# A hybrid attention layer on one Trainium2 core: queries and keys are transposed before they are split, x groups are split later, and the work is dealt anew over ScalarE, VectorE and GpSimd

## The chip, the cores and the metric

The kernel runs as one program on one core of a Trainium2 chip. A core has five engines with a queue of instructions each, worked off in order: TensorE (PE in the profile, with its weight loads as PEld), VectorE (DVE), ScalarE (ACT), GpSimd (POOL), and SyncE (SP), which here issues the DMAs. TensorE reads SBUF and writes PSUM; GpSimd works on SBUF alone in this kernel. The metric is device time in microseconds (us) of one execution; lower is better. Of the kernel before there are three timed runs and one profiled execution.

## The reference

One decoder layer on x of 2048 positions and 1024 channels, in float32:

```python
hdn = rmsnorm(x, norm_gain[i])
proj = jnp.einsum("bsd,de->bse", hdn, w_in[i])
q_a, k_a, v_a, g_a, q_b, k_b, v_b, g_b = jnp.split(proj, split_at, axis=-1)

q_a = rope(rmsnorm(q_a.reshape(b, S, A_HEADS, HEAD_DIM), q_norm_a[i]), pos)
k_a = rope(rmsnorm(k_a.reshape(b, S, A_KV_HEADS, HEAD_DIM), k_norm_a[i]), pos)
v_a = v_a.reshape(b, S, A_KV_HEADS, HEAD_DIM)
o_a, _, _ = banded_attention(q_a, k_a, v_a, A_WINDOW - 1, sinks=sinks_a[i])
o_a = o_a.reshape(b, S, A_WIDTH).astype(x.dtype) * jax.nn.silu(g_a)

q_b = rope(rmsnorm(q_b.reshape(b, S, B_HEADS, HEAD_DIM), q_norm_b[i]), pos)
k_b = rope(rmsnorm(k_b.reshape(b, S, B_HEADS, HEAD_DIM), k_norm_b[i]), pos)
v_b = v_b.reshape(b, S, B_HEADS, HEAD_DIM)
o_b = dilated_attention(q_b, k_b, v_b)
o_b = o_b.reshape(b, S, B_WIDTH).astype(x.dtype) * jax.nn.silu(g_b)

mixed = jnp.concatenate([o_a, o_b], axis=-1)
x = x + jnp.einsum("bse,ed->bsd", mixed, w_out[i])
```

Mixer A has 8 query heads and 2 key heads of 64 channels and looks back 127 positions, with a learned sink per head. Mixer B has 8 heads; each attends under three patterns of window and stride, (128, 1), (512, 4) and (2048, 16), and the three results are merged by their softmax denominators.

## The kernel before

**Split products.** TensorE works in the format fp32r, so every float32 operand is split into a high part h (a ScalarE copy into fp32r) and a low part l (the value less h). A projection product is three matmuls, h*h, h*l and l*h (`mm3`, line L244). A score is two: the stationary operand holds the query's high part in 64 of its 128 partitions and its low part in the other 64; the first moving operand holds the key's high part in both halves (tile `KK`), the second the key's low part in the half that meets the query's high part and zeros elsewhere (tile `KLZ`, in the profile `klz`; L590, L591).

**Stages.** `STAGES` has eight: four of kind B (two heads of mixer B each), two of kind A (four query heads and one key head), two of kind O (half of the output columns each). Every stage goes through 2048 positions as four `sb` of 512 and eight halves `hf` of 256. `proj` does a half: two matmul groups `pj` of 128 positions (`tt`), 24 matmuls of 384 columns each, then one (B) or two (A) gate groups of 24 matmuls of 256 columns. `pj` has two PSUM buffers, which the gates use too.

**x.** `x_load` brings eight of the 16 half groups, two of four x groups, into `xs` in one DMA on SP; `x_split` makes `xh` on ScalarE (L155) and `xl` on GpSimd or VectorE (L157): groups 0 and 1, and all of hf 6 and 7, on GpSimd, the rest on VectorE. The tiles `xh` and `xl` have six buffers each; a half needs four. The next half's groups 0 and 1 are split after this half's first `pj` group, groups 2 and 3 during its last gate group.

**Queries and keys.** `norm_rope` multiplies `pj` by the rope tables on VectorE into `t1` (four buffers) and `t2`, and GpSimd adds them (L430). `norm_split` multiplies by the norm factor (L446) and splits at once, positions still on the partitions: high parts on ScalarE (L455, L456), low parts on GpSimd (L457, L458), all into `hl`. The next half's `finish`, taken from `deferred` after its second `pj` group, calls `qk_transposes`: TensorE transposes blocks of `hl` that pair high and low (L474 and L498 in B, L484, L489 and L490 in A) into PSUM tiles `po`, and ScalarE copies them into `Q`, `qc`, `KK` and `KLZ` (L476, L477, L501; in A L486, L492, L493). In B, GpSimd copies the queries into a second layout `qc`, which goes to DRAM for the strided patterns.

**Attention.** Units of scores, transposes of the probabilities, products with the values and a last step wait in `pending`. `proj` yields an estimated cost after each pair of operations, and the main loop starts the next step of a unit whenever the attention's share of work has fallen behind the projection's. `evac_o` and `pair_units` move the products out of PSUM by a ScalarE copy into `ob` (one buffer) and a VectorE add.

**Order.** The program is written in this order, and a scheduler then orders each engine's queue by its own estimates. So where an instruction stands on its engine is read from the compiled order.

## Time and profile before

| what | value |
|---|---|
| three timed runs, median | 1264.9 us (1262.76 to 1270.4) |
| the profiled execution, its own time | 1271.72 us |
| its span, first to last instruction | 1269.9 us |
| mean granted TensorE clock | 0.97 |
| ScalarE, x splits (L155) | 252 of 627 ns |
| VectorE, x splits (L157) | 94 of 859 ns |
| GpSimd, x splits (L157) | 158 of 1365 ns |

Groups of instructions are told by source line, engine, operation, and the tiles written and read. Busy time is that of the group; the idle time beside it is what its engine stood just before, with what ended it. A matmul's own duration includes its way through the array, so that consecutive ones overlap; what one holds of TensorE is the distance from its start to the next one's. A row of waits names the engine and line that waited, and the one whose end released it.

### The profile page before, as it was taken

The numbers are of one execution on the slowest core, as the hardware profiler recorded it, in microseconds if no ns is written. First come the engines' busy times: TensorE is split into PE (matmuls) and PEld (weight loads), VectorE is DVE, ScalarE is ACT, GpSimd is POOL, SyncE is SP. The second block draws the span as 40 slices with busy tenths as digits, with TensorE's granted clock in tenths as the row PEclk, the third lists the DMA queues.
The fourth block names the chain that finished last, engine by engine and source line by source line (L and its number), as shares of the span: only waits on it lengthen the run. The fifth ranks groups of instructions, "written<-read, shape, count | busy, mean of one in ns | idle before, by whom it ended". The sixth has DMA issues, their size and how long they took to land. (4 is left out here: it accounts for less than half of the span.)

```text
span 1269.9 us, 25442 instructions
## 1 busy us (share of the span) xinstructions
PE 1179.8 (93%) x8328; PEld 1143.5 (90%) x8328; DVE 867.5 (68%) x2288; ACT 837.1 (66%) x2418; POOL 685.3 (54%) x788
## 2 busy tenths in 40 slices
PE   6898979988799898898998999999899999999899
PEld 6798979988699898898997999998799998999898
DVE  5666678776667677776877879888777868622221
ACT  6567777777668587676877767786776877513221
POOL 4876644566454755545676566673556565333122
PEclk9899989999999899898998999999899999999999
DMA  7454678776677776787866775555223235566551
GB/s 215 128 148 114 176 214 243 211 202 185 193 212 232 198 198 181 219 235 197 221 200 191 212 199 150 149 165 165 91 73 109 80 97 157 164 197 205 177 188 70
DMA packets 196883, 220.98 MB, mean 174 GB/s; under 512 B 34312, under 2 KB 143632, under 8 KB 196752
## 3 DMA queue, kind: packets, MB, share of 16 engines
q1 hardware_dynamic: 196752, 219.37, 59.2%
q8 instruction: 66, 1.08, 0.4%
q14 instruction: 65, 0.53, 0.1%
HBM read 164.44 MB, written 54.86 MB: 173 GB/s over the span
## 5 line engine op out<-in xcount | busy, mean ns | idle before, releaser
L244 PE MATMUL pj<-wh,xh 128*128 128x384 f32 (+1 forms) x1008 | 334.1, 334 | 18.6 <-ACT xh L155 6.7
L244 PE MATMUL pj<-wl,xh 128*128 128x384 f32 (+1 forms) x1008 | 334.9, 332 | 1.4 <-DVE wl L102 0.8
L244 PE MATMUL pj<-wh,xl 128*128 128x384 f32 (+1 forms) x1008 | 331.9, 331 | 1.1 <-POOL xl L157 0.8
L157 POOL TENSOR_TENSOR xl<-xs,xh 128x512 fp32r<-128x512 f32 x158 | 213.7, 1365 | 143.8 <-ACT xh L155 139.1
L155 ACT ACTIVATE xh<-xs 128x512 fp32r<-128x512 f32 x252 | 153.5, 627 | 115.8 <-PE pj L244 98.8
L244 PEld LDWEIGHTS pj<-wh,xh 128*128 128x128 f32 x1008 | 194.4, 193 | 22.4 <-ACT xh L155 7.1
L244 PEld LDWEIGHTS pj<-wl,xh 128*128 128x128 f32 x1008 | 194.6, 193 | 3.6 <-DVE wl L102 1.1
L244 PEld LDWEIGHTS pj<-wh,xl 128*128 128x128 f32 x1008 | 194.4, 193 | 3.5 <-DVE xl L157 1.3
L574 DVE TENSOR_TENSOR ptl<-pt,pth 128x512 fp32r<-128x512 f32 (+3 forms) x232 | 141.6, 619 | 42.2 <-ACT pth L573 40.2
L244 PE MATMUL pj<-xh,wgh 128*128 128x256 f32 x496 | 147.1, 297 | 10.7 <-DVE V L310 8.4
L244 PE MATMUL pj<-xh,wgl 128*128 128x256 f32 x496 | 145.3, 293 | 0.0
L244 PE MATMUL pj<-xl,wgh 128*128 128x256 f32 x496 | 144.7, 292 | 0.0
L573 ACT ACTIVATE pth<-pt 128x512 fp32r<-128x512 f32 (+3 forms) x232 | 123.1, 543 | 25.6 <-PE po L645 9.4
L430 POOL TENSOR_TENSOR t<-t,t 128x256 f32<-128x256 f32 (+1 forms) x96 | 79.2, 826 | 80.9 <-DVE t L421 57.2
L244 PEld LDWEIGHTS pj<-xh,wgh 128*128 128x128 f32 x496 | 97.7, 197 | 12.9 <-DVE V L310 5.8
L446 DVE TENSOR_TENSOR t<-t,fac 128x256 f32<-128x256 f32 (+1 forms) x96 | 76.9, 815 | 33.0 <-POOL fac L182 30.1
L244 PEld LDWEIGHTS pj<-xh,wgl 128*128 128x128 f32 x496 | 97.7, 197 | 0.8
L814 ACT ACTIVATE P<-P,scD 128x128 f32<-128x128 f32 (+3 forms) x128 | 71.6, 560 | 40.5 <-DVE scD L813 39.6
L244 PEld LDWEIGHTS pj<-xl,wgh 128*128 128x128 f32 x496 | 97.8, 197 | 0.4
L157 DVE TENSOR_TENSOR xl<-xs,xh 128x512 fp32r<-128x512 f32 x94 | 79.8, 859 | 20.2 <-ACT xh L155 19.8
L182 POOL TENSOR_TENSOR fac<-un,mhalf 128x8 f32<-128x8 f32 (+1 forms) x48 | 85.3, 1778 | 2.7
L599 ACT ACTIVATE P<-P,scA 128x256 f32<-128x256 f32 (+1 forms) x128 | 63.1, 495 | 23.4 <-DVE scA L598 23.0
(188 smaller groups left out, 3087.8 us busy)
## 6 DMA issues: line engine op xcount, KB each, us to landing
xs<-in_xT SPq DMA_DIRECT2D x94, 512.0 KB
xs<-mx SPq DMA_DIRECT2D x32, 512.0 KB
vd<-V SPq DMA_DIRECT2D x64, 128.0 KB
qd<-qc SPq DMA_DIRECT2D x32, 256.0 KB
TT<-tab SPq DMA_DIRECT2D x32, 256.0 KB
cv<-vd SPq DMA_DIRECT2D x32, 256.0 KB
cq<-qd SPq DMA_DIRECT2D x32, 256.0 KB
ck<-kd SPq DMA_DIRECT2D x64, 128.0 KB
```

The costliest lines, as they stand in the source:

```text
L155: nc.scalar.activation(h, f, AF.Copy)
L157: eng.tensor_tensor(l, f, f32(h), op=OP.subtract)
L182: nc.gpsimd.tensor_tensor(y, u, mhalf.to_broadcast([128, n]), op=OP.pow)
L244: nc.tensor.matmul(o, a, b, start=first and n == 0, stop=last and n == 2, skip_group_check=True)
L430: nc.gpsimd.tensor_tensor(t1[:, :n], t1[:, :n], t2[:, :n], op=OP.add)
L446: nc.vector.tensor_tensor(t1v, t1v, fac[:, tt, :, None].to_broadcast([128, nh, 64]), op=OP.mult)
L573: nc.scalar.activation(hi, pt, AF.Copy)
L574: nc.vector.tensor_tensor(lo, pt, f32(hi), op=OP.subtract)
L599: nc.scalar.activation(pd, pd, AF.Exp, bias=nb[i], scale=-1.0, accum_out=l[i])
L814: nc.scalar.activation(pd, pd, AF.Exp, bias=nb, scale=-1.0, accum_out=l)
```

## The change

- `norm_split` is gone. `norm_scale` only multiplies `t1` by the norm factor. The unsplit float32 `t1` of a half's two groups goes to `qk_transposes`, and `t1` is held until then.
- `qk_transposes` transposes `t1` with the float32 identity `idf`: four blocks in B, four and two in A (on `t1`'s 64 key columns). One ScalarE copy stages each PSUM tile in SBUF, in a tile named `ob`, which now has two buffers.
- From the staged tile, ScalarE writes the high queries and both copies of the high keys, VectorE subtracts for the low queries (two instructions in B, four in A), and GpSimd subtracts for the low keys (two).
- In A, the low keys lie in both `KLZ` halves, one for even and one for odd heads, so that two query heads can have their high parts in different partitions; the copies at the border of two `sb` are two there, not one.
- `xh` and `xl` have seven buffers. GpSimd subtracts three of four x groups. Group 1 is split during the second `pj` group, group 2 behind it, group 3 in the last gate group; in the O stages groups 1 to 3 during the second group, and both x loads are issued at the start of a half.
- The yields and the cost table `pcost` are adjusted.

```diff
-XB = 6
+XB = 7
...
-        eng = nc.gpsimd if g < 2 or hf >= 6 else nc.vector
+        eng = nc.gpsimd if g < 3 or hf >= 6 else nc.vector
...
+                    if nx and tt == 1 and c == 3:
+                        x_split(*nx, 1)
                     yield 490
                 if tt == 0 and nx:
                     x_load(*nx, 1)
                     x_split(*nx, 0)
-                    x_split(*nx, 1)
...
                 if tt == 1:
+                    if nx:
+                        x_split(*nx, 2)
...
-                    if nx and gc == ngc - 1 and c in (1, 3):
-                        x_split(*nx, 2 + c // 2)
+                    if nx and gc == ngc - 1 and c == 3:
+                        x_split(*nx, 3)
...
+    def qk_transposes(si, sb, half, t1s):
         KK, KL = K[si, sb]
         q = Q[si, sb]
         i0 = 2 * half
+        lo64, hi64 = slice(0, 64), slice(64, 128)
+
+        def keys(t, h):
+            return t[:, h, :, i0 + 1:i0 + 3, :].rearrange("p r i u -> p i r u")
+
+        def queries(tile, h, src):
+            a, b = (hi64, lo64) if h else (lo64, hi64)
+            o = tile[:, h, i0:i0 + 2, :]
+            nc.scalar.activation(o[a], src[a], AF.Copy)
+            nc.vector.tensor_tensor(o[b], src[a], f32(o[a]), op=OP.subtract)
+
+        def staged(pt):
+            f = wk.tile([128, 2, 2, 128], F32, name="ob", bufs=2)
+            nc.scalar.activation(f, pt, AF.Copy)
+            return f
+
+        if STAGES[si][0] == "B":
+            pt = ps.tile([128, 2, 2, 128], F32, name="po", bufs=2)
+            for b in range(2):
+                for tt, t1 in enumerate(t1s):
+                    nc.tensor.transpose(pt[:, b, tt, :], t1[:, 128 * b:128 * b + 128], idf)
+            F = staged(pt)
+            for h in range(2):
+                queries(q[0], h, F[:, 0])
+            pk = F[:, 1].rearrange("p i (r u) -> p i r u", u=32)
+            for h, (a, b) in enumerate(((lo64, hi64), (hi64, lo64))):
+                nc.scalar.activation(keys(KK, h)[a], pk[a], AF.Copy)
+                nc.scalar.activation(keys(KK, h)[b], pk[a], AF.Copy)
+                nc.gpsimd.tensor_tensor(keys(KL, h)[a], pk[a], f32(keys(KK, h)[a]), op=OP.subtract)
...
+            F = staged(pt)
+            for b in range(2):
+                for h in range(2):
+                    queries(q[b], h, F[:, b])
+            yield 436
+            pt = ps.tile([64, 2, 128], F32, name="po", bufs=2)
+            for tt, t1 in enumerate(t1s):
+                nc.tensor.transpose(pt[:, tt, :], t1[:, 256:320], idf)
+            F = wk.tile([64, 2, 128], F32, name="ob", bufs=2)
+            nc.scalar.activation(F, pt, AF.Copy)
+            pk = F.rearrange("p i (r u) -> p i r u", u=32)
+            for a in (lo64, hi64):
+                nc.scalar.activation(keys(KK, 0)[a], pk, AF.Copy)
+            for h, a in enumerate((lo64, hi64)):
+                nc.gpsimd.tensor_tensor(keys(KL, h)[a], pk, f32(keys(KK, 0)[lo64]), op=OP.subtract)
```

**The order at three places.** The number behind a tile's name tells its instances apart.

TensorE before, in the first A stage, the first gate group of the fifth half (`pj_11365`) and the transposes of split data, of two halves before, that fall into it:

```order
L244 MATMUL pj_11365<-xh_10870,wgh_9598 128x256
L244 MATMUL pj_11365<-xl_10871,wgh_9598 128x256
L244 MATMUL pj_11365<-xh_10870,wgl_9599 128x256
L244 MATMUL pj_11365<-xh_10870,wgh_9607 128x256
L244 MATMUL pj_11365<-xl_10871,wgh_9607 128x256
L489 MATMUL po_10975<-idr_76,hl_10744 128x128
L490 MATMUL po_10975<-idr_76,hl_10744 64x128
L484 MATMUL po_10995<-idr_76,hl_10750 128x128 x4
L719 MATMUL pt_11158<-idf_75,P_11033 128x128 x4
```

TensorE after, at the same place: the last transpose of `t1` from two halves before, and then the gate group (`pj_10944`) of this half:

```order
L495 MATMUL po_10587<-idf_75,t1_10154 64x128
L718 MATMUL pt_10733<-idf_75,P_10622 128x128 x4
L670 MATMUL po_10662<-idf_75,eA_10657 8x128
L807 MATMUL sc_10968<-ck_10758,cq_10756 128x256
L808 MATMUL sc_10968<-cl_10761,cq_10756 128x256
L807 MATMUL sc_10977<-ck_10758,cq_10756 128x384
L808 MATMUL sc_10977<-cl_10761,cq_10756 128x384
L734 MATMUL po_10766<-pth_86,V_9332 128x512
L734 MATMUL po_10781<-pth_86,V_9712 128x512
L734 MATMUL po_10781<-pth_86,V_9815 128x256
L734 MATMUL po_10781<-pth_86,V_9406 128x256
L242 MATMUL pj_10944<-xh_10450,wgh_9206 128x256
```

The gate group stood 11 rows ahead of the key transposes (L489, L490); now it begins 11 rows behind them (L495). The rope products of this half, which have to be done before that PSUM buffer is used again, write a `t1` buffer that these transposes read.

VectorE before, in the first A stage, at the rope products (L426, L428) of the sixth half's first 128 positions:

```order
L412 TENSOR_REDUCE un_11556<-sq_11675 128x5
L426 TENSOR_TENSOR t1_11679<-pj_11557,TT_11265 128x256
L428 TENSOR_TENSOR t2_11680<-pj_11557,TT_11265 128x256
L426 TENSOR_TENSOR t1_11679<-pj_11557,TT_11265 128x64
L428 TENSOR_TENSOR t2_11680<-pj_11557,TT_11265 128x64
L310 SCALAR_TENSOR_TENSOR V_11674<-pj_11557,rst_83,V_11674 128x64
```

VectorE after, at the rope products (L427, L429) of the same positions:

```order
L459 TENSOR_TENSOR Q_9920<-ob_10908,Q_9920 64x256 x2
L459 TENSOR_TENSOR qc_9921<-ob_10908,qc_9921 64x256
L427 TENSOR_TENSOR t1_11240<-pj_11122,TT_10836 128x256
L429 TENSOR_TENSOR t2_11241<-pj_11122,TT_10836 128x256
L427 TENSOR_TENSOR t1_11240<-pj_11122,TT_10836 128x64
L459 TENSOR_TENSOR qc_9921<-ob_10908,qc_9921 64x256
L429 TENSOR_TENSOR t2_11241<-pj_11122,TT_10836 128x64
L311 SCALAR_TENSOR_TENSOR V_11235<-pj_11122,rst_82,V_11235 128x64
```

The low queries (L459, four instructions of 64x256) of the half two before now stand before and between the rope products.

ScalarE before, in a B stage, the four x splits (`xh`, L155) of one half among the exponentials (L599):

```order
L155 ACTIVATE xh_6424<-xs_6326 128x512
L599 ACTIVATE P_6270,scB_6068<-P_6270,scB_6068 128x256 x2
L155 ACTIVATE xh_6434<-xs_6326 128x512
L599 ACTIVATE P_6270,scB_6068<-P_6270,scB_6068 128x256 x2
L155 ACTIVATE xh_6590<-xs_6470 128x512
L155 ACTIVATE xh_6594<-xs_6470 128x512
```

ScalarE after, at the like place (x splits L153, exponentials L598, tanh of the gates L335, the staging copy L463):

```order
L153 ACTIVATE xh_6180<-xs_6074 128x512
L598 ACTIVATE P_6018,scB_5830<-P_6018,scB_5830 128x256 x2
L153 ACTIVATE xh_6326<-xs_6206 128x512
L598 ACTIVATE P_6018,scB_5830<-P_6018,scB_5830 128x256 x2
L153 ACTIVATE xh_6364<-xs_6206 128x512
L335 ACTIVATE gz_6197<-G_5630 128x256
L565 ACTIVATE ob_5973<-po_5964 64x512
L463 ACTIVATE ob_6138<-po_6133 128x512
```

The four splits of one half stood within six rows, the third and fourth directly behind one another. Now the first group's split stands nine rows ahead of these rows, and the rows show groups 1, 2 and 3, each with other work between.

More of the change, by code (lines that the diff above doesn't have):

```diff
@@ L50, in hybrid_layer @@
     idf = const.tile([128, 128], F32, name="idf")
-    idr = const.tile([128, 128], F32R, name="idr")
     mk = const.tile([128, 768], F32, name="mk")
@@ L78, in late_constants @@
         nc.sync.dma_start(idf, ident)
-        nc.scalar.activation(idr, idf, AF.Copy)
         nc.sync.dma_start(mk, masks)
@@ L348, in finish @@
                 nc.scalar.activation(KK[:, h, :, 0, :], f32(pk[:, h, :, 4, :]), AF.Copy)
-            for h in range(nk):
+            for h in range(2):
                 hs = slice(64 * h, 64 * h + 64)
                 nc.scalar.activation(KL[hs, h, :, 0, :], f32(pl[hs, h, :, 4, :]), AF.Copy)
-        yield from qk_transposes(si, sb, half, hls)
+        yield from qk_transposes(si, sb, half, t1s)
         if half == 0:
@@ L466, in qk_transposes @@
         i0 = 2 * half
-        for tt, hl in enumerate(hls):
-            i = i0 + tt
-            if kind == "B":
-                blocks = [hl[:, 2 * b:2 * b + 2, :] for b in range(4)]
-                pt = ps.tile([128, 4, 128], F32R, name="po", bufs=2)
-                for b, a in enumerate(blocks):
-                    nc.tensor.transpose(pt[:, b, :], a, idr)
-                pv = f32(pt).rearrange("p h (r u) -> p h r u", u=32)
-                nc.scalar.activation(q[0][:, :, i, :], f32(pt)[:, 0:2], AF.Copy)
-                nc.scalar.activation(KK[:, :, :, i + 1, :], pv[:, 2:4], AF.Copy)
+        lo64, hi64 = slice(0, 64), slice(64, 128)
@@ L495, in qk_transposes @@
[L495 to L503 removed]
+            yield 436
+        else:
+            pt = ps.tile([128, 2, 2, 128], F32, name="po", bufs=2)
+            for b in range(2):
+                for tt, t1 in enumerate(t1s):
+                    nc.tensor.transpose(pt[:, b, tt, :], t1[:, 128 * b:128 * b + 128], idf)
+            F = staged(pt)
+            for b in range(2):
+                for h in range(2):
+                    queries(q[b], h, F[:, b])
+            yield 436
+            pt = ps.tile([64, 2, 128], F32, name="po", bufs=2)
+            for tt, t1 in enumerate(t1s):
+                nc.tensor.transpose(pt[:, tt, :], t1[:, 256:320], idf)
[6 more added lines that the diff above has]
+                nc.gpsimd.tensor_tensor(keys(KL, h)[a], pk, f32(keys(KK, 0)[lo64]), op=OP.subtract)
+            yield 218
@@ L564, in evac_o @@
     def evac_o(po, dst):
-        ob = wk.tile([64, 512], F32, name="ob", bufs=1)
+        ob = wk.tile([64, 512], F32, name="ob", bufs=2)
         nc.scalar.activation(ob, po[64:128, :], AF.Copy)
```

67 lines of the change are left out of this document (12 added, 55 removed).

## The prediction

> **What bounds the kernel now.** I read the page's busy line first, then the stretches of the program, then who waited for whom on the way to TensorE, then the groups of instructions by shape.
>
> The page's line of each engine's busy time, share of the span and instructions:
>
> ```profile
> PE 1179.8 (93%) x8328; PEld 1143.5 (90%) x8328; DVE 867.5 (68%) x2288; ACT 837.1 (66%) x2418; POOL 685.3 (54%) x788
> ```
>
> TensorE (PE) is busy for 93% of the 1269.9 us span, and 90.1 us are left. The same by stretches, each row with the length, then PE, weight loads, VectorE (DVE), ScalarE (ACT) and GpSimd (POOL): the four B stages, the two A stages, a full piece of the A stages, the two O stages (cut at about where the kind changes).
>
> ```profile
> 0.00:673.00 673.00, 609.04 (x4060) 589.20 (x4061) 480.14 (x1262) 486.01 (x1394) 390.34 (x491) 0.95 0.69 196
> 673.00:1045.00 372.00, 356.65 (x2522) 343.53 (x2521) 300.96 (x847) 272.77 (x841) 226.68 (x242) 0.98 0.48 140
> 770.00:820.00 50.00, 48.77 (x355) 46.94 (x354) 44.88 (x133) 38.79 (x125) 33.83 (x38) 1.00 0.52 151
> 1045.00:1270.00 225.00, 214.11 (x1750) 210.76 (x1748) 86.41 (x182) 78.29 (x185) 68.25 (x55) 1.00 0.52 164
> ```
>
> The B stages leave PE 64.0 us idle, the A stages 15.4. In the A stages DVE is the next engine: 81% (300.96 of 372), and 90% from 770 to 820 us, where PE still ran at 98%. So time that leaves PE's queue shortens the program, and DVE decides how much of it in A. The waits that bear on this change, with us in total, times and longest:
>
> ```profile
> POOL xl L157 <- ACT xh L155: 139.1, 37, 9.7
> ACT xh L155 <- PE pj L244: 98.8, 62, 7.4
> PE po L474 <- POOL hl L457: 7.9, 7, 2.0
> PE po L484 <- POOL hl L457: 1.1, 1, 1.1
> PE po L498 <- ACT KK L477: 6.4, 2, 5.5
> PE sc L591 <- ACT klz L501: 1.3, 2, 1.1
> ```
>
> ACT stands 98.8 us, in its order, for PE to free an `xh` buffer, and POOL behind it 139.1; PE itself stands 9.0 us for the low halves that POOL makes ahead of the transposes.
>
> **PE: the transposes.** A B half of 256 positions has 10 transposes of split data before (32 halves), an A half 12 (16 halves): 512. After, 4 and 6 of unsplit f32: 224. What one holds of PE's time is read from the timeline, start to start, with the tail that shows in the longer first matmul behind a run:
>
> ```profile
> 301.62 0.47 PE L474 MATMUL po<-idr,hl 128*128 128x128 f32 x4
> 301.92 0.33 PE L498 MATMUL po<-idr,hl 128*128 128x128 f32 x2
> 302.09 0.35 PE L808 MATMUL sc<-ck,cq 128*128 128x256 f32 x1
> 302.28 0.28 PE L809 MATMUL sc<-cl,cq 128*128 128x256 f32 x1
> ...
> 1089.22 0.28 PE L244 MATMUL pj<-wgh,xl 128*128 128x256 f32 x1
> 1089.34 1.03 PE L719 MATMUL pt<-idf,P 128*128 128x128 f32 x8
> 1090.13 0.37 PE L590 MATMUL sc<-KK,qc 128*128 128x256 f32 x1
> 1090.33 0.28 PE L591 MATMUL sc<-klz,qc 128*128 128x256 f32 x1
> ```
>
> A 256-column matmul takes 0.12 us (1089.22 to 1089.34). Six split transposes: 302.28 - 301.62 - 0.12 = 0.54, 0.090 each. Eight unsplit: 1090.33 - 1089.34 - 0.12 = 0.87, 0.109 each. An unsplit one is dearer, but 512 x 0.090 = 46.1 and 224 x 0.109 = 24.4: **PE loses 21.7 us**, 32 x 0.46 = 14.9 of it in B (0.90 - 0.436 a half) and 16 x 0.43 = 6.8 in A. Nothing hides it where PE is full, so it counts whole.
>
> **DVE: the low queries.** The rows by shape (count, busy us, mean ns, idle before):
>
> ```profile
> L740 DVE TENSOR_TENSOR osum<-po,ob 64x256 f32<-64x256 f32 x64 | 26.4, 413 | 3.6 <-ACT ob L737 3.1
> L331 DVE TENSOR_TENSOR G<-pj,RB 128x256 f32<-128x256 f32 x62 | 25.6, 413 | 5.5 <-PE pj L244 5.4
> L335 DVE SCALAR_TENSOR_TENSOR G<-gz,G 128x256 f32<-128x256 f32 x64 | 47.5, 742 | 9.3 <-ACT gz L334 9.1
> L446 DVE TENSOR_TENSOR t<-t,fac 128x256 f32<-128x256 f32 x64 | 54.1, 860 | 27.8 <-POOL fac L182 27.2 <-POOL t L430 0.6
> L157 DVE TENSOR_TENSOR xl<-xs,xh 128x512 fp32r<-128x512 f32 x94 | 79.8, 859 | 20.2 <-ACT xh L155 19.8
> ```
>
> Sixty-four partitions cost as much as 128 (413 and 413). But with both tensors in SBUF the same 256 elements take 742 and 860, not 413. The change adds 2 such subtractions per B half and 4 per A half: 32 x 2 + 16 x 4 = 128 of 64x256, both inputs in SBUF. I take 0.742, the row that also follows an ACT copy directly: 95.0 us; the ends are 0.413 (52.9) and 0.860 (110.1). The third x group of hf below 6 leaves DVE: 6 x 8 - 1 = 47 instructions (half of the 94) x 0.859 = 40.4. Net +54.6 (12.5 to 69.7). In A: 64 x 0.742 - 12 x 0.859 = +37.2, 301 to 338 of 372, or 91%.
>
> By the Trainium skill ("SBUF — State Buffer", section "SBUF: two separate sides") GpSimd and a two-SBUF-input VectorE instruction take a shared port pair as an exclusive lock for a whole instruction. The gap of 329 ns between the L335 and L331 rows agrees with it. By it the change works against itself, giving both engines more of just such work; as an estimate from that page, a wait of half a POOL split at POOL's 57% share, 0.39 us, would make the 128 cost 103 us in place of 95, which leaves the sum as it is and adds to the first rival below.
>
> **POOL and ACT.** Their rows:
>
> ```profile
> L157 POOL TENSOR_TENSOR xl<-xs,xh 128x512 fp32r<-128x512 f32 x158 | 213.7, 1365 | 143.8 <-ACT xh L155 139.1 <-DMA TT<-tab 2.2
> L457 POOL TENSOR_TENSOR hl<-t,hl 128x128 fp32r<-128x128 f32 x64 | 32.3, 504 | 13.7 <-ACT hl L455 12.2 <-PE pj L244 1.3
> L458 POOL TENSOR_TENSOR hl<-t,hl 128x128 fp32r<-128x128 f32 x64 | 31.5, 492 | 1.5 <-ACT hl L456 0.9 <-PE po L849 0.6
> L457 POOL TENSOR_TENSOR hl<-t,hl 128x256 fp32r<-128x256 f32 x32 | 26.9, 842 | 17.8 <-ACT hl L455 17.8
> L458 POOL TENSOR_TENSOR hl<-t,hl 128x64 fp32r<-128x64 f32 x32 | 13.1, 411 | 0.0
> L566 ACT ACTIVATE ob<-po 64x512 f32<-64x512 f32 x64 | 38.1, 595 | 15.3 <-PE po L849 8.3 <-PE po L645 5.8
> L456 ACT ACTIVATE hl<-t 128x256 fp32r<-128x256 f32 x64 | 26.0, 407 | 0.3
> L455 ACT ACTIVATE hl<-t 128x128 fp32r<-128x128 f32 x64 | 19.4, 303 | 9.7 <-DVE t L446 7.6 <-PE po L498 1.9
> L476 ACT ACTIVATE Q<-po 128x256 fp32r<-128x256 f32 x64 | 24.2, 378 | 11.4 <-PE po L474 11.1
> L477 ACT ACTIVATE KK<-po 128x256 fp32r<-128x256 f32 x64 | 24.5, 383 | 0.0
> L501 ACT ACTIVATE klz<-po 64x256 fp32r<-64x256 f32 x64 | 24.0, 376 | 3.3 <-PE po L498 2.7
> ```
>
> POOL loses 32.3 + 31.5 + 26.9 + 13.1 = 103.8 us of splits. It gains 96 low-key subtractions (2 a half) of 64x256. No row has that shape there; between 0.504 (128x128, 48.4) and 0.842 (128x256, 80.8) I take the second, since on DVE fewer partitions saved nothing. With 47 x 1.365 = 64.2 for x: +41.2 (8.8 to 41.2), 685 to 726, 57%: not a bound. As an estimate, the Trainium skill ("GPSIMD Engine Reference", section "1. Specifications") also speaks for the upper end, each core owning 16 partitions; no run here shows it.
>
> ACT per B half: before 2 x (0.303 + 0.407 + 0.378 + 0.383 + 0.376) = 3.69; after one staging copy (0.595) and six of 64x256 (0.407): 3.04. That is -21 us over B, off the path; an A half goes from 12 instructions to 8, and six boundary copies of 64x128 come in A, each under the 0.376 of 64x256. It pays only through ACT's order.
>
> **Waits.** The 9.0 us for POOL's low halves lose their cause: f32 `t1` goes straight into the transposes. The 6.4 on L498 was for a third `po` buffer in the half; one is used now. Something else will be late there; I take half, 3.2. Together -12.2 (0 to -15.4).
>
> New is what lies between the transposes and the scores: staging, two query and four key copies on ACT, then POOL: 0.595 + 6 x 0.407 + 0.842 = 3.88 us, where the low keys took 2 x 0.376 = 0.75. PE stood 1.3 us for that copy; stretched by 3.88/0.75 that is 6.7, so +5.4 (0 to 22, the third rival).
>
> New too: `t1` is held until its transposes. It has four buffers, so the rope products of half n+2 wait for the transposes of half n. In stage A0 the order puts these behind the projection of half n+2, with 11 rows of other PE work before the gates that need the rope's PSUM buffer back. The four query subtractions stand on DVE among these rope products: 4 x 0.742 = 2.97 us a half. If those 11 rows and what PE still has queued hide all but 0.4 us, 16 halves cost +6.4 (0 to 47.5).
>
> **x groups.** A seventh buffer and later splits let the third x group be written before the gates, not in them. I count nothing for it, as PE hardly waited for x itself; its worth is the second rival. Two things I count at nothing: the staged tile shares `ob`, held until the subtractions are done, with the copies of the PV products, and ACT stands in order behind a missing one; the second buffer covers that, and if it doesn't, each case costs up to POOL's 0.842. In the O stages the second x load is issued on SP at the start of a half, ahead of the residual loads and stores; it waits there for the half before's last split, and PE's queue of 96 matmuls x 0.12 us per 128 positions covers it.
>
> **Sum** against the profiled execution's own 1271.7 us: -21.7 - 12.2 + 5.4 + 6.4 = -22.1, which is 1249.6. That execution lies 6.8 above the median of the three runs (1264.9), so the forecast is **1243**; its own range is 1229 (no new wait, all of the old gone) to 1261.
>
> **Rivals.**
>
> 1. *Slower: DVE in A.* None of the 2.97 us is hidden: 16 x 2.97 = 47.5 in place of 6.4, and the forecast becomes 1243 + 41 = 1284. For it: DVE would be at 91% over all of A, as in the full piece alone now (90%), and L335's lock-like waits. Against: in those 50 us PE ran at 98%. From 21.7/16 = 1.36 us standing a half it eats PE's saving, from about 2.1 us the kernel is over 1% slower. Chance 0.14.
> 2. *Much faster.* ACT's 98.8 us behind `xh` is what makes the B stages' other inputs late. If a third of their 64.0 idle us goes as well, 1243 - 21 = 1222. For it: the 139.1 us behind it on POOL. Against: only a few us of PE's own waits name x. Chance 0.17.
> 3. *No change.* The keys, now last on POOL behind 1.365 us x splits, are late for each new key tile: 24 x 0.9 us = 22 in place of 5.4, and, with the old waits replaced by others, 1243 + 17 + 5 = 1265. For it: POOL waits and works in order. Against: POOL has 43% left. Chance 0.20.
>
> That the change doesn't do what it says is ruled out by the order of instructions.
>
> **Chances and range.** The forecast has 0.49. About 1% (12.6 us) is what runs that spread from 1262.8 to 1270.4 can tell from no change. Faster by over 1%: the second rival and three quarters of the forecast, 0.54; within 1%: the rest of it and most of the third, 0.31; slower: 0.15. The range 1216 to 1274 leaves out the first rival and the far end of the second.
>
> **What would show it.** 224 transposes at 0.109 with no wait on POOL; DVE's L459 rows near 742 ns (413: no contention; above 860: the first rival), and DVE at 90% in A; ACT's wait on `pj` for `xh` well under 98.8; few us of PE on the low-key subtraction (L478, L502). PE idle time over 90 us would prove me wrong; if it sits before the A gates, by the first rival, if before the scores, by the third.

## The result and the profile after

The changed kernel takes 1284.29 us (median, 1282.82 to 1286.01), the kernel before 1265.95 on the same chip: a ratio of 1.0124 (95% interval 1.0086 to 1.0162). It is slower by 1.2%, where 1243 us was forecast. The profiled execution took 1282.82 us and spans 1281.1. Its line of busy times:

```profile
PE 1171.1 (91%) x8040; PEld 1121.3 (88%) x8040; DVE 913.9 (71%) x2369; ACT 839.7 (66%) x2263; POOL 724.1 (57%) x739
```

The 288 matmuls less are there (8328 to 8040), but PE's idle time grew from 90.1 to 110.0 us. The stretches are cut here where the first projection matmul of the first A and the first O stage starts; the columns are those of the prediction, and the last three are the granted clock, the DMA's share and GB/s. First the kernel before, then the changed one:

```profile
0.00:672.00 672.00, 608.20 (x4056) 588.52 (x4056) 479.29 (x1260) 485.01 (x1391) 390.34 (x491) 0.95 0.69 196
672.00:1058.00 386.00, 369.59 (x2617) 355.86 (x2617) 314.71 (x885) 284.49 (x876) 233.29 (x248) 0.98 0.47 139
1058.00:1270.00 212.00, 202.01 (x1658) 199.11 (x1656) 73.49 (x145) 67.57 (x153) 61.63 (x49) 1.00 0.53 169
```

```profile
0.00:657.00 657.00, 592.73 (x3861) 564.86 (x3862) 498.88 (x1297) 481.19 (x1291) 410.56 (x454) 0.97 0.71 200
657.00:1057.00 400.00, 370.45 (x2533) 352.55 (x2533) 343.06 (x931) 291.37 (x823) 237.10 (x225) 0.98 0.45 134
1057.00:1281.00 224.00, 207.96 (x1651) 203.85 (x1649) 71.92 (x143) 67.13 (x151) 76.46 (x61) 0.96 0.52 159
```

The B stages won 15 us. The A stages lost 14, and PE's idle time there grew by 13. The O stages lost 12: 6 more of PE standing, and the rest as matmuls at a lower clock. The granted clock fell from 1.00 to 0.96 there; from 1180 to 1185 us, where it was 0.50, a 256-column matmul came every 0.21 us, and every 0.12 where it was 1.00. The waits of the changed kernel that the prediction spoke of:

```profile
POOL xl L155 <- ACT xh L153: 199.1, 63, 8.5
ACT xh L153 <- DMA xs<-in_xT: 77.2, 33, 5.4
ACT xh L153 <- PE pj L242: 67.4, 26, 9.9
ACT xh L153 <- DMA xs<-mx: 46.7, 12, 9.4
```

The row to see is the second with the fourth. ScalarE, in its order, now stands 124 us for x loads that have not landed; before it was 8.3. What that does to TensorE is seen in one piece of a B stage (timeline of the changed kernel; in brackets the idle time just before, and what ended it):

```profile
405.02 0.60 ACT L565 ACTIVATE ob<-po 64x512 f32<-64x512 f32 x1 [1.42 <-PE po L848]
405.72 0.38 SPq L146 DMA_DIRECT2D xs<-in_xT  x1
...
411.02 0.63 ACT L153 ACTIVATE xh<-xs 128x512 fp32r<-128x512 f32 x1 [5.41 <-DMA xs<-in_xT]
411.68 0.49 ACT L572 ACTIVATE pth<-pt 128x384 fp32r<-128x384 f32 x1
...
412.06 0.59 ACT L463 ACTIVATE ob<-po 128x512 f32<-128x512 f32 x1
412.20 0.56 DVE L573 TENSOR_TENSOR ptl<-pt,pth 128x384 fp32r<-128x384 f32 x1 [2.58 <-ACT pth L572]
...
412.22 0.50 PE L644 MATMUL po<-pth,V 128*128 128x256 f32 x2 [0.81 <-ACT pth L572]
```

The load is issued at 405.72. ACT has nothing left to do at 405.61 but the copy of that load, and stands until 411.02. Behind it in its queue are the split of the probabilities (L572) and the staging copy (L463). VectorE stands 2.58 us for the first of them and TensorE 0.81. The row of TensorE names `pth`; the cause is the x copy in front of it.

In the O stages ACT stands for x too, up to 9.43 us, but another queue is late there as well. SP issues the next x loads in a pair, then stores a result, and stands until the store has landed, 8 us later; only then does it issue the second O stage's weights (L116). The changed kernel, then the one with six buffers (below) at the like place:

```profile
1163.22 0.85 SPq L146 DMA_DIRECT2D xs<-mx  x2
1164.13 0.42 SPq L560 DMA_DIRECT2D out<-cq  x1
1172.39 0.33 SPq L512 DMA_DIRECT2D cq<-in_x  x1
1172.77 0.43 SPq L560 DMA_DIRECT2D out<-cv  x1
1173.30 0.38 SPq L116 DMA_DIRECT2D stg<-in_wO  x1
```

```profile
1138.44 0.34 SPq L560 DMA_DIRECT2D out<-cq  x1
1139.69 0.32 SPq L146 DMA_DIRECT2D xs<-mx  x1
1141.15 0.33 SPq L512 DMA_DIRECT2D cq<-in_x  x1
1144.21 0.34 SPq L560 DMA_DIRECT2D out<-cv  x1
1144.75 0.46 SPq L116 DMA_DIRECT2D stg<-in_wO  x1
```

The stage's first matmul was at 1170.7 and at 1149.0, so the weights were asked for 2.6 us behind it and not 4.3 ahead. TensorE then stood 6.3 us for their copies (`wh`, L99), 1.1 with six buffers.

### The profile page after: what moved, and what is told of

Read it like the earlier page. It is cut to its first block, busy times and chain, and to the rows that moved or that the text cites. A ratio compares the mean times of both kernels' runs of the same rounds, so it can differ in the third digit from the quotient of the medians.

```text
span 1281.1 us, 24644 instructions
## 1 busy us (share of the span) xinstructions
PE 1171.1 (91%) x8040; PEld 1121.3 (88%) x8040; DVE 913.9 (71%) x2369; ACT 839.7 (66%) x2263; POOL 724.1 (57%) x739
## 4 chain that ended last, share of the span: by engine, by line
PE 27%; DMA 25%; DVE 19%; ACT 15%; issue 6%; POOL 6%; SPq 2%; POOLq 0%; DVEq 0%; ACTq 0%
PE pj L242 19%; DMA xs<-in_xT 8%; DVE ptl L573 2%; ACT pth L572 2%; DMA stg<-in_wB 2%; ACT xh L153 2%; ACT P L598 2%; DVE P L597 2%; DMA rD<-rr 2%; DVE t L444 2%; DMA Rb<-rD 2%; DVE Q L459 1%; DMA out<-cq 1%; POOL xl L155 1%; ACT P L813 1%
## 5 line engine op out<-in xcount | busy, mean ns | idle before, releaser
L155 POOL TENSOR_TENSOR xl<-xs,xh 128x512 fp32r<-128x512 f32 x205 | 276.4, 1360 | 200.9 <-ACT xh L153 199.1
L153 ACT ACTIVATE xh<-xs 128x512 fp32r<-128x512 f32 x252 | 153.5, 625 | 200.0 <-DMA xs<-in_xT 77.2
L572 ACT ACTIVATE pth<-pt 128x512 fp32r<-128x512 f32 (+3 forms) x232 | 121.9, 537 | 6.4 <-DVE ptl L573 3.6
L598 ACT ACTIVATE P<-P,scA 128x256 f32<-128x256 f32 (+1 forms) x128 | 63.0, 494 | 18.2 <-DVE scA L597 17.9
L242 PE MATMUL pj<-wgl,xh 128*128 128x256 f32 x248 | 71.8, 290 | 2.3 <-DVE wgl L100 2.3
```

What stands on the lines that cost most here:

```text
L153: nc.scalar.activation(h, f, AF.Copy)
L155: eng.tensor_tensor(l, f, f32(h), op=OP.subtract)
L242: nc.tensor.matmul(o, a, b, start=first and n == 0, stop=last and n == 2, skip_group_check=True)
L572: nc.scalar.activation(hi, pt, AF.Copy)
L598: nc.scalar.activation(pd, pd, AF.Exp, bias=nb[i], scale=-1.0, accum_out=l[i])
```

## The experiments

Each kernel is the changed one or the kernel before with some steps undone or added. The qk path is the new way of queries and keys; the sibling of a kernel is the one that it differs from by the edit named. Times are medians, and ratios are against the kernel before in the same comparison (its median there was 1268 to 1270 us).

**Which part.** Theories at the start: T1, two causes, the x places in O (13 us) and the qk path in A (19); T2, the x groups are to blame everywhere; T3, the qk path alone.

The qk path alone, all of the x part undone:

```diff
-XB = 7
+XB = 6
-        eng = nc.gpsimd if g < 3 or hf >= 6 else nc.vector
+        eng = nc.gpsimd if g < 2 or hf >= 6 else nc.vector
...
```

> The changed kernel with the whole x part undone: six xh and xl buffers, two of four groups on GpSimd, the old places of the splits and of the x loads in all stages. What is left is the new way of queries and keys. By the count of projection matmuls, the changed kernel's extra TensorE idle time is 0 us in the B stages, 19 in the A stages and 13 in the O stages. Theory 1 (two causes: the O part of the x change costs the 13 us, the new query and key path costs the 19 in A): O goes back to about 12.6 us idle, A stays near 48, the kernel comes to 1284 - 13 = about 1271. Theory 2 (the x change is to blame everywhere, since ScalarE waits 77 us for x from DMA where it waited 8): A and O both go back, about 1252. Theory 3 (the query and key path alone): no change, about 1284.

Measured 1267.6 us, 0.9999 (0.9977 to 1.0021): the loss is gone, and so is the gain. Two causes seemed nearest. Then the O stages' loads and splits alone put back:

```diff
-                x_load(*nx, 1)
-                    if nx and tt == 1 and c in (1, 3, 5):
-                        x_split(*nx, 1 + c // 2)
+                    if nx and tt == 1 and c in (1, 3):
+                        x_split(*nx, 2 + c // 2)
...
```

> The changed kernel with the x loads and splits of the O stages alone put back: second load after the first group, groups 0 and 1 after it, groups 2 and 3 in the second group. Theories 1 and 2: the 13 us of O come back, about 1271. If O's loss comes from what the A stages leave over, or from chance in the order: about 1284.

1284.5 us, 1.0152 (1.0114 to 1.0190): not the O stages' text. The third group back on VectorE:

```diff
-        eng = nc.gpsimd if g < 3 or hf >= 6 else nc.vector
+        eng = nc.gpsimd if g < 2 or hf >= 6 else nc.vector
```

> The changed kernel with the third x group of hf below 6 back on VectorE, all else as changed. It gives VectorE 47 x 0.81 = 38 us back and takes 47 x 1.36 = 64 us from GpSimd. If GpSimd's queue is what is late (the low keys behind x splits): faster, 5 to 15 us, with the 10.9 us that TensorE and ScalarE stand for the low keys of A halved. If VectorE's load bounds A: slower by 5 to 10 us. If neither: within 3 us of the changed kernel.

1291.0 us, 1.0196 (1.0165 to 1.0228): GpSimd is not to blame either. It is slower than the changed kernel by 7 us, as was expected if VectorE's load bound the A stages, so that is asked next. The low queries from the PSUM tile in place of the staged one:

```diff
-            nc.vector.tensor_tensor(o[b], src[a], f32(o[a]), op=OP.subtract)
+            nc.vector.tensor_tensor(o[b], psrc[a], f32(o[a]), op=OP.subtract)
...
```

> The changed kernel, but the low queries are subtracted from the transposes in PSUM, not from their staged copy in SBUF, so that these 128 instructions no longer have both inputs in SBUF. By the shared-port reading they fall from 614 and 710 ns to about 413, VectorE loses some 29 us, and if VectorE in the A stages is what costs the 19 us there (my first rival), the kernel gets faster by 8 to 15 us. If VectorE's load is not it: within 3 us of the changed kernel, or slower by a few, as the PSUM buffer is held longer.

1279.3 us, 1.0095 (1.0068 to 1.0122). The subtraction fell from 614 and 710 ns to 422 (rows in the last section), 28 us less on these rows; other rows of VectorE grew, and its whole busy time fell by 18.5 (913.9 to 895.4). The program gained 5 us at most, and the two intervals overlap.

**Which stage.** Theories: P, the later places help B and hurt A; L, chance of the order, tied to no stage; S, the seven buffers cost everywhere. New places and the third group on GpSimd in B only:

```diff
+        eng = nc.gpsimd if g < (3 if STAGES[si][0] == "B" else 2) or hf >= 6 else nc.vector
+                    if nx and kind == "B" and tt == 1 and c == 3:
...
```

> The changed kernel with the new places of the x splits and the third x group on POOL kept in the B stages only; A and O stages have the old places, the old engine for the third group and the old loads, seven buffers stay. Theory P (place: the later splits help the B stages and hurt the A stages): the stages of the traces so far add to 652 (B, as in the changed kernel) + 382 (A, as in the kernel with the qk path alone) + 217 (O, as there) + 5 = 1256 us against a before of about 1267, a ratio near 0.99, and PE idles near 100 in B and 31 in A. Theory L (the lines are drawn by chance of the order, and no stage carries the cost of its own edits): a time between that of the kernel with the qk path alone and the changed kernel, 1267 to 1284, with A's idle not tied to A's places. Theory S (seven buffers and their layout cost everywhere): as the changed kernel, 1284.

1268.0 us, 1.0011 (0.9989 to 1.0033), where P wanted 1256. The first A stage, with its old text, took 212 us, as in the changed kernel (211), and 200 with the qk path alone: the cost is not tied to the text of the stage, which is against P. The mirror (the same edit with "A"):

> The mirror: new places and third group on POOL in the A stages only, old ones in B and O. Theory P: 664 (B, as with the qk path alone) + 400 (A, as in the changed kernel) + 217 + 5 = 1286 us, slower than before by 1.5 per cent, and PE idles 45 to 50 us in the A stages. Theory L: 1267 to 1284 and no tie to A. Theory S: 1284.

1292.4 us, 1.0191 (1.0168 to 1.0215). The time is nearest P's 1286, but not for P's reason: its B stages, with old text, were as long as the slowest seen (670 us), where P wanted 664, and its A stages took 393, where P wanted 400. The B variant with the low queries from PSUM:

> As the kernel with the new places in the B stages only, and the low queries subtracted from the PSUM tile and not from its staged copy (0.42 us in place of 0.61 and 0.71 us each on DVE, 27 us less DVE work in all). Theory P: DVE's load is what the A stages idle on, so 0.3 to 0.5 per cent below its sibling, about 1251 us; this would beat both kernels. Theory L: no difference from its sibling beyond 0.3 per cent either way. Theory S: 1279, as the changed kernel with this edit.

1275.4 us, 1.0054 (1.0035 to 1.0073): slower than its sibling, not faster. So less work on VectorE did not help here; the edit also changes the order and how long the PSUM tile is held. Last, the qk path with the third group on GpSimd, old places, six buffers:

```diff
 XB = 6
-        eng = nc.gpsimd if g < 2 or hf >= 6 else nc.vector
+        eng = nc.gpsimd if g < 3 or hf >= 6 else nc.vector
```

> The qk path alone with old places and six buffers, and the third x group on POOL in all stages: the engine by itself, without the places. Theory P: POOL is not what the A stages wait for and DVE gets some 32 x 0.8 = 26 us back, so at or below the qk path alone, 1258 to 1268 us. Rival (POOL's queue ahead of the low keys and the rstd chain): slower than the qk path alone by 5 to 10, 1273 to 1278 us, with more of PE's waits on POOL.

1255.3 us, 0.9902 (0.9881 to 0.9924): faster than before, and 29 us faster than the changed kernel, from which it differs by the places of the splits, the O loads, and the seventh buffers. It is called the fast sibling from here on.

**The buffer.** Theory B: the seventh buffer lets the scheduler put ScalarE's copies earlier, where they stand for the load. The fast sibling with seven buffers:

```diff
-XB = 6
+XB = 7
```

> The qk path with old places and the third x group on POOL (1255 us in the last comparison), with seven in place of six buffers for the x groups and nothing else. The program text is the same, but the scheduler writes another order with it. Theory B (the seventh buffer lets the scheduler put the split's copy earlier in ACT's order, where it stands for the x load): slower than its sibling by 10 to 25 us, 1265 to 1280, and ACT's wait for the x loads goes from 20 us to 70 or more. Theory P (the places of the splits cost, the buffer does not): as its sibling, 1250 to 1259, and the wait stays at 20 to 30.

1289.2 us, 1.0150 (1.0125 to 1.0174): 34 us for one constant, 31 by the ratios, and more than was expected. The waits with six, then with seven:

```profile
ACT xh L153 <- PE pj L242: 98.7, 48, 9.5
ACT xh L153 <- DMA xs<-in_xT: 20.2, 6, 9.6
ACT xh L153 <- DMA xs<-mx: 2.4, 1, 2.4
```

```profile
ACT xh L153 <- DMA xs<-in_xT: 92.6, 38, 9.6
ACT xh L153 <- DMA xs<-mx: 64.6, 14, 9.6
ACT xh L153 <- PE pj L242: 50.0, 24, 9.8
```

By stages: with six, 97.0 of the 98.7 us lie in the O stages. There ACT waits until PE gives an `xh` buffer back, and by then x has landed. In the B and A stages it hardly waits for a buffer (1.7 us), and 20.2 us for x. With seven it waits 92.6 us for x in B and A, and 64.6 in O. In B and A, then, the ring of six acts not by a wait but through the order. The traces show it: ACT runs the same 2263 instructions, and the x copies (252, taken in their order) stand 7.4 places earlier among them on average with seven buffers than with six.

The same with the O stages' new loads and splits (the O lines of the change's diff):

> As the sibling with seven buffers, and the O stages' x loads and splits as in the changed kernel (both loads at the start of the half, splits spread). With this, what is left to the changed kernel are the later splits in the B and A stages. If the O places cost (theory of the first comparison, 12 us at most in the stage table): slower than the sibling with seven buffers by 5 to 12 us. If they cost nothing, as putting them back in the changed kernel suggests: within 3 us of that sibling.

1291.6 us, 1.0174 (1.0151 to 1.0198), 2 us off its sibling: the new places of the O loads in the text cost nothing. (With seven of both, SP issues two O loads one behind the other with the old text too.) Two by the side; the third group on GpSimd in the kernel before, and the low queries from PSUM in the fast sibling:

> The kernel before, with the third x group on POOL as its one change: what that part is worth without the qk path. If the engine of the third group is what made the qk path pay (the qk path alone gave nothing, with it 13 us less), DVE's 40 us of relief is worth little in the kernel before, where DVE carries no low queries: 1261 to 1268 us. If the third group pays by itself, whatever the qk path: about 13 us less, 1255.

> The qk path with the third x group on POOL, and the low queries subtracted from the PSUM tile and not from its staged copy. If DVE's load in the A stages still costs PE there (17 us of idle in each), 27 us less on DVE give 0.3 to 0.6 per cent on its sibling: 1248 to 1252 us, the fastest so far. If what is left is the order of the scheduler: within 0.3 per cent of the sibling either way.

1269.4 us, 1.0010 (0.9987 to 1.0034), and 1256.3 us, 0.9908 (0.9878 to 0.9938). Neither gives anything.

**Order or memory.** Theory M: the memory with seven buffers costs, not the order. The seventh buffer for `xh` alone, then for `xl` alone:

```diff
-        h = xp.tile([128, 2, 256], F32R, name="xh", bufs=XB)
+        h = xp.tile([128, 2, 256], F32R, name="xh", bufs=7)
...
```

> The qk path with the third x group on POOL and old places (1255 us), a seventh buffer for the high halves xh alone, six for the low halves. The compiled order changes on all five engines. Theory B: 1280 to 1290 us, ACT's wait for x loads 100 us or more. Theory M (the memory or the number of semaphore slots with seven buffers, not the order): 1255 to 1275, half of the loss at most.

```diff
-        l = xp.tile([128, 2, 256], F32R, name="xl", bufs=XB)
+        l = xp.tile([128, 2, 256], F32R, name="xl", bufs=7)
...
```

> The same with the seventh buffer for the low halves xl alone: the compiled order of every engine is the same, row for row, as with six; only the buffers differ. Theory B: as the sibling with six, 1252 to 1260 us. Theory M: slower by a part of the 34 us, 1265 to 1289.

1287.2 us, 1.0141 (1.0095 to 1.0187) for `xh`, and 1258.4 us, 0.9927 (0.9896 to 0.9958) for `xl`, whose compiled order is the sibling's. M falls. Their waits for x, `xh` first:

```profile
ACT xh L153 <- DMA xs<-in_xT: 89.3, 37, 9.3
ACT xh L153 <- DMA xs<-mx: 43.0, 13, 5.4
```

```profile
ACT xh L153 <- DMA xs<-in_xT: 17.0, 6, 9.6
```

Any other order might cost as much, so the fast sibling with another order and six buffers:

```diff
-    pcost = {"B": 4 * 8 * 490 + 2 * 8 * 330 + 2 * 436, "A": 4 * 8 * 490 + 4 * 8 * 330 + 2 * 654, "O": 4 * 8 * 650}
+    pcost = {"B": 4 * 8 * 490 + 2 * 8 * 330 + 4 * 340, "A": 4 * 8 * 490 + 4 * 8 * 330 + 4 * 340, "O": 4 * 8 * 650}
```

> A disturbance of the order that takes no work away and adds no buffer: in the qk path with the third group on POOL, the two numbers for the cost of a slot in the table pcost are the old ones (4 x 340 in place of 872 and 1308). The order differs in 3328 rows of PE's list. Theory C (any other order costs some per cent, and the fast sibling is a lucky one): 1265 to 1290 us. Theory B: the x copies stay where they are, so within 8 us of the sibling, 1248 to 1263.

1259.1 us, 0.9933 (0.9900 to 0.9966): this other order costs 4 us at most, not 30; it is one order, not any. Then the changed kernel itself, with that one constant put back:

```diff
-XB = 7
+XB = 6
```

> The changed kernel with one constant put back: six buffers for the x groups in place of seven; later splits, third group on POOL, O loads and the whole qk path stay. Theory B (the seventh buffer changes the order that the scheduler writes, ACT's x copies come earlier and stand for the x loads): 1250 to 1265 us, faster than before, and ACT's wait for x loads falls from 124 us (77 and 47) to below 40. Theory P (with it the later places cost as well): 1265 to 1280.

**1251.1 us, 0.9861 (0.9824 to 0.9897)**, faster than the kernel before and the changed one, and with the lowest time of the kernels that do all the work (its interval overlaps that of the fast sibling). The later splits, the O loads, GpSimd's third group and the qk path are all in it. Its stretches and waits:

```profile
0.00:650.00 650.00, 591.54 (x3866) 568.37 (x3866) 512.51 (x1298) 483.88 (x1300) 413.13 (x453) 0.97 0.71 203
650.00:1037.00 387.00, 368.27 (x2526) 353.07 (x2527) 349.98 (x934) 289.48 (x816) 237.26 (x226) 0.98 0.47 138
1037.00:1249.00 212.00, 203.62 (x1650) 200.06 (x1648) 72.80 (x139) 68.70 (x150) 77.26 (x61) 0.99 0.52 168
```

```profile
ACT xh L153 <- PE pj L242: 97.8, 51, 7.4
...
ACT xh L153 <- DMA xs<-in_xT: 9.9, 5, 4.2
ACT xh L153 <- DMA xs<-mx: 4.0, 2, 2.7
```

Against the kernel before: B 22 us shorter, A 1 longer, O the same. Against six buffers, then, the seventh costs 7 us in B, 13 in A and 12 in O. ACT's waits for x in the changed kernel are spread another way: 59 us in B, 18 in A, 47 in O.

**The loads.** Does the order with seven cost because of the loads, or by what the early copies push back? The x loads of the B and A stages left out, with seven buffers and with six (all later halves of these stages then compute with the x of the first half):

```diff
+        if STAGES[si][0] != "O":
+            XS[si, hf, g] = XS[0, 0, g]
+            return
...
```

> The changed kernel, seven buffers, with the x loads of the B and A stages left out: after the first half every split reads the one x tile that is there already (so all later halves compute with the x of the first; the O stages load as ever). The splits, their copies on ACT and all later work stay. Theory B with the loads as its cause (a load takes about 5 us from its issue, and ACT comes to the copy too early for it): with no load to stand for, seven buffers cost no more than 1 per cent over six, both at 1225 to 1255 us. Theory B without it (ACT's earlier copies hurt by what they push back in ACT's order, landed or not): seven stays 15 to 35 us slower than six.

> The same with six buffers: the other half of the pair. ACT's wait for x loads was 10 us there, so taking the loads away gives little, 1235 to 1252 us; the difference of the two against the 33 us that the seventh buffer costs with loads is the share that the loads carry.

1230.8 us, 0.9710 (0.9685 to 0.9735) with seven, 1236.2 us, 0.9741 (0.9712 to 0.9769) with six. Without these loads seven buffers are, if anything, better: the loss needs the loads. Two things limit this. Leaving the loads out reorders every engine, so these are not the two orders of before; but the early places are kept: the x copies stand 8.2 places earlier on ACT with seven than with six, and 7.6 earlier with the loads. And it takes 49 of 221 MB off the DMA queues, in both kernels alike; the one with six buffers got 15 us faster by it, where its ACT had stood 10 us for these loads. That the loads cost by ACT's standing in B and A, and by SP's queue as well in O, is read from the waits and the timelines; neither was varied by itself.

**All kernels in one table.** The last three columns are from the traces: ACT's wait for x loads (the L153 or L155 rows, from `in_xT` and `mx`, added); how long after the issue of a load on SP ACT had worked off all that stands ahead of that load's first copy, as the median of 126 loads; and for how many of them that was under 6 us.

| kernel | `xh` buffers | ratio to before | ACT's wait for x, us | ACT comes after, us | under 6 us |
|---|---|---|---|---|---|
| before | 6 | 1 | 8 | 12.3 | 15 |
| before, third on GpSimd | 6 | 1.0010 | 16 | 12.0 | 17 |
| qk path alone | 6 | 0.9999 | 22 | 12.9 | 20 |
| qk, third on GpSimd | 6 | 0.9902 | 23 | 12.5 | 19 |
| the same, other `pcost` | 6 | 0.9933 | 23 | 12.4 | 21 |
| the same, seven `xl` | 6 | 0.9927 | 17 | 12.3 | 19 |
| the same, queries from PSUM | 6 | 0.9908 | 25 | 11.7 | 22 |
| **changed, six buffers** | 6 | 0.9861 | 14 | 11.3 | 19 |
| new x in B only | 7 | 1.0011 | 145 | 6.7 | 55 |
| the same, queries from PSUM | 7 | 1.0054 | 162 | 6.4 | 59 |
| changed, queries from PSUM | 7 | 1.0095 | 145 | 6.6 | 57 |
| **changed** | 7 | 1.0124 | 124 | 6.3 | 59 |
| qk, third on GpSimd, seven `xh` | 7 | 1.0141 | 132 | 5.5 | 66 |
| the same, seven of both | 7 | 1.0150 | 157 | 5.7 | 66 |
| changed, old O | 7 | 1.0152 | 145 | 6.4 | 59 |
| seven of both, new O | 7 | 1.0174 | 144 | 5.7 | 66 |
| new x in A only | 7 | 1.0191 | 113 | 6.7 | 60 |
| changed, third on VectorE | 7 | 1.0196 | 146 | 5.8 | 64 |

Where ACT stood over 0.3 us for a load in the changed kernel (44 times), the copy began 3.9 to 6.8 us after the issue, at the median 5.0. With six buffers ACT comes 11 to 13 us after the issue, well after the landing; with seven 5.5 to 6.7, and for about half of the loads too early. No kernel lies between the groups. Within the seven-buffer group the wait's size does not rank the times: it says nothing of what stands behind the copy at each place, and the `mx` part belongs to the x of the O stages, where ACT has little else to do and SP's queue, shown above, is late as well.

## Why the prediction was wrong

**The step that failed** is "x groups. A seventh buffer and later splits let the third x group be written before the gates, not in them. I count nothing for it". It is worth +33 us (1284.3 against 1251.1), from the seventh buffer; in the fast sibling the one for `xh` alone cost as much as both, and the one for `xl` nothing. The other item that it counted at nothing, the O stages' loads on SP, cost nothing with six buffers; with the order of seven, SP came late with the weights. The prediction asked whether PE waits for x. It did not ask what kept ACT's copies behind the loads: the ring of six did, in the O stages by ACT's wait for a free buffer, in B and A through the order that the scheduler writes with it. It also read the order only at the transposes and the scores, and not where the x copies stand on ACT and how far behind SP's issue that is.

**The same with the 98.8 us.** The second rival took ACT's wait for `xh` buffers as a cost in B. The kernel before, from 1050 to 1270 us:

```profile
ACT xh L155 <- PE pj L244: 91.1, 44, 7.4
```

Nearly all of it lay in the O stages, where ACT has little else to do. That wait was harmless, and in these stages it was the guard against the other one.

**PE's saving: right.** Four unsplit transposes, from the timeline of the changed kernel:

```profile
271.14 0.60 PE L470 MATMUL po<-idf,t 128*128 128x128 f32 x4
271.50 0.36 PE L242 MATMUL pj<-xl,wgh 128*128 128x256 f32 x1
271.70 0.28 PE L242 MATMUL pj<-xh,wgl 128*128 128x256 f32 x1
```

271.70 - 271.14 - 0.12 = 0.44, or 0.110 each (0.109 taken). Over all runs of four transposes at full clock, the median is 0.109 each after, and 0.091 before (0.090 taken). The count is as forecast, so by these prices PE's work falls by about 21.8 us, where -21.7 was forecast. There is no wait on POOL ahead of the transposes.

**The rest of the sum: near the forecast where ACT does not stand for x, in part by luck.** With six buffers, and idle time taken as a stage's length less its matmuls at those prices, against the kernel before: B -7.3 us (99.6 to 92.3), A +7.4 (28.7 to 36.1), O +1.5. The forecast's -12.2 + 5.4 + 6.4 is -0.4; measured is +1.6. The spans differ by 20.1 us where the sum says 22.1, and the ratio 0.9861 on 1264.9 us is 1247, with 1243 inside its interval (1242.6 to 1251.9). But what this calls idle time holds the clock too. In B the granted clock was 0.95 before and 0.97 with six buffers: the traces' clock rows put 61 and 42 us of it at half clock, where matmuls start further apart. As an estimate from how much further, that alone is 7 us, as much as the whole -7.3; PE's own standing fell by 5, and other delays grew by about as much. The forecast had no term for the clock. Single terms may be off against each other as well; that `t1` is held, and that `ob` is shared, was not tested alone. (The low end of the forecast's own range, 1229, is 1228 by its terms.)

**DVE, POOL, ACT.** The rows of the changed kernel by shape:

```profile
L459 DVE TENSOR_TENSOR Q<-ob,Q 64x256 fp32r<-64x256 f32 x96 | 58.9, 614 | 7.2 <-ACT Q L458 4.2
L459 DVE TENSOR_TENSOR qc<-ob,qc 64x256 fp32r<-64x256 f32 x32 | 22.7, 710 | 1.0
L478 POOL TENSOR_TENSOR klz<-ob,KK 64x256 fp32r<-64x256 f32 x64 | 50.7, 792 | 20.9 <-ACT KK L476 18.7
L502 POOL TENSOR_TENSOR klz<-ob,KK 64x256 fp32r<-64x256 f32 x32 | 26.7, 836 | 5.2 <-ACT KK L500 4.0
L590 PE MATMUL sc<-klz,Q 128*128 128x256 f32 x192 | 51.7, 291 | 7.4 <-POOL klz L502 5.2 <-POOL klz L478 2.2
```

The low queries took 81.6 us, not 95; the low keys 0.792 and 0.836, where 0.842 was taken; PE stood 7.4 us for them, 1.3 + 5.4 forecast. So the third rival did not happen. ACT's 21 us in B did not show: its busy time went from 837.1 to 839.7 (last section). PE idle time over 90 us was the prediction's own sign of being wrong, and it came to 110.0.

**The first rival** had the right sign, near the right time (1284), and the wrong cause. PE's idle time in the A stages did grow, by 13 us. But with six buffers DVE is busy 349.98 of 387 us there, 90%, and PE idles 18.7 us, against 16.4 before. And 19 us less on DVE in the fast sibling (930.0 to 910.9) changed nothing (0.9908 against 0.9902).

**Open.** Moving the third group to GpSimd gives 12 us on the qk path (0.9999 to 0.9902), and nothing on the kernel before. By the profiles they lie in B (669.8 to 652.2 us), where DVE is not full; whether it is the engine or the order that comes with it was not told apart. Open too is by which path the seventh buffer costs 13 us in A, where ACT stands only 18 us for x, and why the kernel with the new x in B only is at 1.0011 and the other seven with seven buffers and the staged queries at 1.012 to 1.020. A seventh buffer in the kernel before was not tried: its SBUF has no room for one.

## What to carry to other kernels

A buffer count is not only room: where a scheduler orders the queues, a full ring of buffers may be what keeps a copy behind the load that it needs. One more buffer then brings the copy forward in an in-order queue, and everything behind it stands for the DMA. So before a ring is made larger, compare how long after a load's issue the first reader's turn comes with how long the load takes; and when a wait for a buffer goes, look at what that engine waits for next.

## What the runs showed of the hardware

**Two inputs in SBUF.** With its first input read from PSUM, the same VectorE subtraction takes (low queries from PSUM, by shape):

```profile
L459 DVE TENSOR_TENSOR Q<-po,Q 64x256 fp32r<-64x256 f32 x96 | 40.5, 422 | 13.9 <-ACT Q L458 10.9
L459 DVE TENSOR_TENSOR qc<-po,qc 64x256 fp32r<-64x256 f32 x32 | 13.5, 422 | 1.0
```

422 ns for both, against 614 and 710 with both inputs in SBUF: 0.19 and 0.29 us an instruction. These means are mixtures. Of the 96 in the changed kernel, the 40 during which GpSimd ran nothing took 418 to 423 ns; the other 56 took 418 to 1510, at the median 664. With one input in PSUM all 96 took 417 to 427, whatever GpSimd did. The Trainium skill ("SBUF — State Buffer", section "SBUF: two separate sides") has a VectorE instruction with two SBUF inputs and a GpSimd instruction that reads SBUF exclude each other for the whole of an instruction. The trace agrees: the excess is there only with two SBUF inputs, and only beside GpSimd.

**ScalarE copies in a row.** Pairs in the timeline, of the changed kernel and of the one with six buffers:

```profile
773.18 0.85 ACT L458 ACTIVATE Q<-ob 64x256 fp32r<-64x256 f32 x2
```

```profile
773.41 1.14 ACT L153 ACTIVATE xh<-xs 128x512 fp32r<-128x512 f32 x2
```

Two x copies of 0.625 us take 1.14, so the second starts before the first ends. Two query copies of 0.412 take 0.85, with no overlap. Single durations therefore overstate what some copies hold of ACT and not others, and that is why a saving counted in durations did not show. In B the copies of queries and keys add up to 112.3 us before and 92.5 after; counted only up to the start of ACT's next instruction, they hold 89.9 and 89.3. What makes the difference was not tested.

**A load's time.** A 512 KB x load was there about 5 us after its issue (3.9 to 6.8 where ACT stood for it in the changed kernel).
